# A hybrid attention and convolution block: the second output projection reads convolution features first, and the second attention runs ahead of the first output projection's sums

## The chip, the cores and the metric

The kernel runs on one core of one Trainium2 chip. The time is device time in microseconds (us) of one execution, and the median of several executions is compared. The engines are named as in the profile: PE is TensorE (PEld its weight loads), DVE is VectorE, ACT is ScalarE, POOL is GpSimd, SP is SyncE. SP issues nearly all transfers here; its row in a profile is SPq.

## The reference

One decoder layer of a Hymba-like block, for 2048 positions and a model width of 1024. One input projection feeds two mixers: gated linear attention (4 heads, keys of 64, values of 128, chunks with a state carried from one to the next) and a gated short convolution of width 3. Their outputs, 512 columns each, go side by side through one output projection and are added to the input; then come a gated FFN (width 2816) and a last norm. What matters here, from the reference:

```
h = rmsnorm(x, norm1_g[l]);  proj = h @ w_in[l]
p_q, p_k, p_v, p_g, p_a, c_b, c_c, c_h = jnp.split(proj, splits, axis=-1)
...
o = gla_chunked(q, k, v, log_a)
o = rmsnorm(o, gla_norm_g[l]).astype(x.dtype)
o = o * jax.nn.silu(p_g.reshape(bsz, seq, GLA_HEADS, GLA_DV))
o_gla = o.reshape(bsz, seq, GLA_WIDTH)
u = c_c * c_h
o_conv = c_b * causal_depthwise_conv(u, conv_w[l])
...
x = x + jnp.concatenate([o_gla, o_conv], axis=-1) @ w_out[l]
```

The output projection sums over 1024 input features: eight blocks of 128, of which blocks 0 to 3 are the attention's heads and blocks 4 to 7 the convolution's features.

## The kernel before

**Numbers.** Each float32 operand is split into a high and a low part that TensorE multiplies at its fast rate, and each product of two tiles is three matmuls: high by high (L496), high by low (L497), low by high (L498). The split is an ACT copy (L198) and a DVE subtraction (L199). Most projections use Strassen's seven products on 2 by 2 blocks (`unit`, `PRODUCTS`); their sums are made on DVE (L448, L530, L364) and ACT.

**Tiling.** The 2048 positions are four blocks of 512 columns. Blocks 0 and 1 are the first half, blocks 2 and 3 the second. A matmul is 128x128 by 128x512.

**Stages.** Input projection of the first half, then of the second (`in_proj(1)`, twelve units of seven products), then the first half's output projection (`first_out_proj`), then the second half's (`out_proj`, from 665.57 us in the profiled execution), then the FFN of each half. The first output projection goes through the output rows in four passes, d0 = 0, 2, 4, 6; each makes seven Strassen products on the convolution features and then plain matmuls on the attention heads (L1386, L1392), and adds all to the residual with `plus` (L1355). The second one uses plain matmuls alone (L1421, L1422, L1424). Its operands are 16 tiles `op` of 0.5 MB, eight blocks of features by two blocks of positions, loaded by `build_mix` from `sgla2`, `sgla3` (attention) and `sm2`, `sm3` (convolution); both are stored in DRAM earlier. Each of its weight tiles `raw` is 1 MB, four quarters, and each quarter is split into one of four `wq` buffers. While it runs, `h2_first` makes the norm's factors of the first half's result (sum by ones on PE, L218; root on ACT, L259; refinement on DVE, L261 and L210 to L212) and the FFN's operands from it (L939, L364, L199).

**Work beside the products.** A list `background` of generators is run by `tick()`, which a unit calls once for each product and the output projections at places of their own. It takes one step at every second call. While `hasty` is set, by `hastened(steps, n)` for the first n steps, it takes one at every fourth call besides, so three of four. The attention of a half, `gla_half`, is such a generator. It goes through 8 chunks of 128 positions, in these steps: `gla_fetch` (14 loads: kq, ee, vt, gt), `gla_scaled` (L1161 to L1164), `gla_scores` (PE L1174, masked copy on DVE L1177, transposes L1180, L1183), `gla_outputs` (PE L1199, L1206, L1214; state on DVE L1224, L1225; head norm L1231 to L1240), `gla_finish` (transpose L1249, gate L1250, split, two stores to `sgla`). The first half's attention is `hastened(gla_half(0), 14)` and runs beside the second half's input projection; the second half's is appended in the middle of that projection, after its silu units, and goes on into the first output projection.

**What sets the order.** The program is written in the order of stages and steps, and the framework then sets each engine's order from that program, its own simulation of when things are ready, and the buffers. `behind(marks)` ties an instruction behind others on its engine: with `behind(last_out + last_plus)` an attention split comes behind the last sums that the product loop has written so far. `plus` renews these marks at each sum. SP issues in order, and each transfer waits for the one eight before it. The operand tiles share 28 buffers, so a load of a new tile waits for the matmuls that read an old one.

Of the kernel before, what the change touches and what calls it, by code (L numbers as in the profile page):

```python
# [25 lines left out]
KD = D // P  # L26
# [4 lines left out]
GROUPS = (0, 2, 5, 8)  # L31
LAST_GROUP = GROUPS[-1]
EARLY = 7
EPS = 1e-6


# [17 lines left out]
def tile_hymba_block(ctx, tc, x, xt, win, wa, wgu, wout, wffn, wdown, wdown_first, small, out):  # L54
# [1022 lines left out]
    def in_proj(half, ops, raw=None, between=(), rest=None):  # L1077
        def units():
            if half == 0:
                yield unit(win[2], ops, raw=raw, between=between, rest=rest)  # L1080
            for u in range(0 if half else 3, 12):
                yield unit(win[u], ops, after=2 if half and u < 3 else None)

        units = units()
        for dst, i0 in ((s_kq, 0), (s_kq, 2), (s_v, 0), (s_v, 2)):
            if half == 0 and dst is s_kq:
                continue
            for r, j, c, p in next(units):
                store(dst[2 * half + j][i0 + r][:], settled(c, p)[:])
        for i0 in (0, 2):  # L1090
            for r, j, c, p in next(units):
                store(s_g[2 * half + j][i0 + r][:], silu(c, p)[:])
        if half:
            background.append(gla_half(half))
        for i0 in (0, 2):
            cc = {(r, j): settled(c, p) for r, j, c, p in next(units)}
            ch = {(r, j): c for r, j, c, _ in next(units)}
            for r in range(2):
                i = i0 + r
                left = halo[:, i, :]  # L1100
                for j in range(2):
                    s = tp.tile([P, PB + 2], F32, name="u", tag="t")
                    dve.tensor_tensor(s[:, 2:], ch[r, j][:], cc[r, j][:], ALU.mult)
                    act.activation(s[:, 0:2], left, AF.Copy)
                    left = s[:, PB : PB + 2]
                    y = cc[r, j]
                    act.activation(y[:], s[:, 0:PB], AF.Copy, scale=col(C_CW + i))
                    for n in (1, 2):
                        dve.scalar_tensor_tensor(
                            y[:], s[:, n : n + PB], col(C_CW + 4 * n + i), y[:], ALU.mult, ALU.add  # L1110
                        )
                if half == 0:
                    act.activation(halo[:, i, :], left, AF.Copy)
            for r, j, c, _ in next(units):
                y = cc[r, j]
                dve.tensor_tensor(y[:], c[:], y[:], ALU.mult)
                dst = s_mix[2 * half + j][i0 + r]
                if half:
                    pair_out(y, dst)
                else:  # L1120
                    store(dst[:], y[:])
# [136 lines left out]
    def plain_weights(src, n):  # L1258

        raw = rawp.tile([P, 4, PB], F32, name="raw", tag="raw")  # L1260
        load(raw[:, 0:n, :], src)
        for i in range(n):
            h = weight_quarter(raw[:, i, :])
            for k in range(4):
                yield h[:, 0, k * P : (k + 1) * P], h[:, 1, k * P : (k + 1) * P]
# [69 lines left out]
    def first_out_proj(y, conv, heads):  # L1335

        ssq = [
            tiny.tile([P, PB], F32, name=f"ssx{j}", tag=f"ssx{j}", bufs=1) for j in range(2)
        ]
        for d0 in range(0, KD, 2):  # L1340
            raw = raw_weights(wout[d0 // 2]).rearrange("p a (b e c) -> p (a b) e c", e=2, c=P)
            quads = [raw[:, k : k + 2, e, :] for e, k in ((0, 4), (0, 6), (1, 6), (1, 4))]
            w = unit_weights(None, quads)
            wh = [weight_quarter(raw[:, 0:HEADS, e, :]) for e in range(2)]

            def mul(i, o=None):
                first = o is None
                o = bank() if first else o
                n, m = PRODUCTS[i]
                for k in range(2):  # L1350
                    product_step(o, w[n], conv[m], k, first)
                return o

            def plus(at, o):
                last_plus[:] = [dve.tensor_tensor(y[at][:], o[:], y[at][:], ALU.add)]  # L1355
                last_out[:] = last_plus
                all_plus.extend(last_plus)

            oa = mul(0)
            plus((0, 0), oa)  # L1360
            ob = mul(1)
            plus((1, 1), ob)
            due("T3")
            tick()
            mul(2, oa)
            plus((0, 1), oa)
            due("B22")
            o = mul(3)
            tick()
            mul(4, oa)  # L1370
            plus((1, 1), oa)
            due("T4")
            mul(5, ob)
            plus((0, 1), ob)
            tick()
            mul(6, oa)
            plus((1, 0), oa)
            tick()
            following = residual(d0 + 2) if d0 + 2 < KD else None
            for e in range(2):  # L1380
                po = [bank() if e or j else o for j in range(2)]
                for k in range(HEADS):
                    c = slice(k * P, (k + 1) * P)
                    for j in range(2):
                        for part in range(2):
                            pe.matmul(  # L1386
                                po[j][:], wh[e][:, 0, c], heads[k][j][:, part, :],
                                start=k + part == 0 and e + j > 0, stop=False,
                                skip_group_check=True,
                            )  # L1390
                    for j in range(2):
                        pe.matmul(  # L1392
                            po[j][:], wh[e][:, 1, c], heads[k][j][:, 0, :], start=False,
                            stop=k == HEADS - 1, skip_group_check=True,
                        )
                    if k % 2:
                        tick()
                for j in range(2):
                    plus((e, j), po[j])
                    store(s_x1[j][d0 + e][:], y[e, j][:])  # L1400
                    sum_squares(ssq[j], y[e, j][:], d0 + e == 0)
            y = following
        return ssq

    def build_mix():
        def pair(b, k):
            return load_pair(s_gla[b][:, k] if k < HEADS else s_mix[b][k - HEADS])

        return [[pair(2 + j, k) for j in range(2)] for k in range(KD)]

    def out_proj(ops, ahead, rest):
        ssq, half = [], 1
        ws = chain.from_iterable(plain_weights(wout[u], 4) for u in range(4))
        for d0 in range(0, KD, 2):
            o = {(e, j): bank() for e in range(2) for j in range(2)}
            for k in range(KD):
                for e in range(2):
                    wh, wl = next(ws)
                    for j in range(2):
                        m = ops[k][j]  # L1420
                        pe.matmul(o[e, j][:], wh, m[:, 0, :], start=k == 0, stop=False)  # L1421
                        pe.matmul(o[e, j][:], wh, m[:, 1, :], start=False, stop=False)  # L1422
                    for j in range(2):
                        pe.matmul(  # L1424
                            o[e, j][:], wl, ops[k][j][:, 0, :], start=False, stop=k == KD - 1
                        )
                if k == 3:
                    ys = {}
                    for e in range(2):
                        for j in range(2):  # L1430
                            ys[e, j] = tt("y")
                            load(ys[e, j][:], xt[2 * half + j, :, d0 + e, :])
                for _ in range(1 if d0 == KD - 2 else 2):
                    next(rest if d0 == KD - 2 else ahead, None)
                tick()
            if d0 == 0:
                ssq += [
                    tiny.tile([P, PB], F32, name=f"ssx{j}", tag=f"ssx{j}", bufs=1)
                    for j in range(2)
                ]  # L1440
            for e in range(2):
                for j in range(2):
                    b, dt = 2 * half + j, d0 + e
                    y = ys[e, j]
                    dve.tensor_tensor(y[:], y[:], o[e, j][:], ALU.add)
                    store(s_x1[b][dt][:], y[:])
                    sum_squares(ssq[j], y[:], dt == 0)
        return ssq
# [506 lines left out]
```

## Time and profile before

| | |
|---|---|
| runs (us) | 2042.27, 2048.67, 2047.19 |
| median (us) | 2047.19 |
| the profiled execution (us) | 2047.66 |
| its span (us) | 2045.9 |
| mean granted TensorE clock | 0.995 |
| PE busy | 2021.6 us, 99% |
| DVE, ACT, POOL busy | 76%, 48%, 1% |
| DMA moved | 429.35 MB, 210 GB/s on average |

A line of a wait table gives the waiting engine, tile and line, the releaser, and then total us, number of times and the longest. A row of a timeline is start, duration, engine, line, operation and tiles; "x4" joins neighbours of one kind, and the bracket at its end is the idle time before it and what ended it. A row by windows gives busy us and counts of each engine, then PEclk, the share of full speed that the clock throttle granted, then DMA share and GB/s. Matmuls overlap, so one of 390 ns ends well after the next has begun.

### The profile page before, as it was taken

The numbers are of one execution on the slowest core, as the hardware profiler recorded it, in microseconds if no ns is written. First come the engines' busy times: TensorE is split into PE (matmuls) and PEld (weight loads), VectorE is DVE, ScalarE is ACT, GpSimd is POOL, SyncE is SP. The second block draws the span as 40 slices with busy tenths as digits, with TensorE's granted clock in tenths as the row PEclk, the third lists the DMA queues.
The fourth block names the chain that finished last, engine by engine and source line by source line (L and its number), as shares of the span: only waits on it lengthen the run. The fifth ranks groups of instructions, "written<-read, shape, count | busy, mean of one in ns | idle before, by whom it ended". The sixth has DMA issues, their size and how long they took to land.

```text
span 2045.9 us, 27026 instructions
## 1 busy us (share of the span) xinstructions
PE 2021.6 (99%) x9275; PEld 1658.7 (81%) x9275; DVE 1563.3 (76%) x2837; ACT 973.5 (48%) x1941; POOL 10.3 (1%) x17
## 2 busy tenths in 40 slices
PE   9999999999999999999999999999999999999998
PEld 8788878787877788888888888887888888888886
DVE  7888877668867597778777688887777777778886
ACT  6664455755534244444444453334444444454345
POOL 0000000000000000000000000000000000000001
PEclk9999999999999999999999999999999999999999
DMA  7356886644684893445445576577454444486653
GB/s 262 122 201 220 283 302 190 196 134 157 229 296 160 323 326 140 170 169 207 171 168 195 184 294 240 189 279 294 150 180 170 153 151 170 166 334 226 247 216 129
DMA packets 194634, 429.35 MB, mean 210 GB/s; under 512 B 20448, under 2 KB 67776, under 8 KB 185024
## 3 DMA queue, kind: packets, MB, share of 16 engines
q1 hardware_dynamic: 193776, 426.97, 58.9%
q8 instruction: 73, 1.20, 0.2%
q10 hardware_dynamic: 720, 0.66, 0.1%
q14 instruction: 65, 0.53, 0.1%
HBM read 279.69 MB, written 147.85 MB: 209 GB/s over the span
## 4 chain that ended last, share of the span: by engine, by line
PE 89%; DMA 5%; DVE 3%; ACT 2%; issue 1%; SPq 1%; POOL 0%; POOLq 0%; DVEq 0%; ACTq 0%
PE mm L496 26%; PE mm L498 26%; PE mm L497 26%; PE mm L1421 1%; PE mm L1424 1%; PE mm L1422 1%; DMA raw<-in_win_dram 1%; DMA op<-shT 1%; PE a_ps L1020 1%; PE mm L801 1%; PE mm L803 1%; PE mm L802 1%; PE mm L1741 1%; PE mm L1386 1%; PE o_ps L1199 1%
## 5 line engine op out<-in xcount | busy, mean ns | idle before, releaser
L496 PE MATMUL mm<-op,wq 128*128 128x512 f32 x2499 | 974.3, 393 | 4.1 <-ACT wq L198 1.5
L497 PE MATMUL mm<-op,wq 128*128 128x512 f32 x2499 | 972.3, 390 | 0.6 <-DVE op L199 0.5
L498 PE MATMUL mm<-op,wq 128*128 128x512 f32 x2499 | 962.1, 390 | 0.3
L198 ACT ACTIVATE wq<-raw 128x512 fp32r<-128x512 f32 (+2 forms) x628 | 361.8, 581 | 599.5 <-PE mm L498 477.6
L496 PEld LDWEIGHTS mm<-op,wq 128*128 128x128 f32 x2499 | 469.5, 188 | 107.6 <-ACT wq L198 4.6
L498 PEld LDWEIGHTS mm<-op,wq 128*128 128x128 f32 x2499 | 469.5, 188 | 99.9 <-DVE wq L199 1.9
L497 PEld LDWEIGHTS mm<-op,wq 128*128 128x128 f32 x2499 | 469.8, 188 | 98.6 <-DVE op L199 2.6
L199 DVE TENSOR_TENSOR wq<-raw,wq 128x512 fp32r<-128x512 f32 (+2 forms) x628 | 389.8, 625 | 165.2 <-ACT wq L198 163.6
L530 DVE TENSOR_TENSOR c<-mm,c 128x512 f32<-128x512 f32 x196 | 134.6, 687 | 71.8 <-PE mm L498 67.1
L530 DVE TENSOR_TENSOR y<-mm,y 128x512 f32<-128x512 f32 x185 | 126.5, 687 | 54.1 <-PE mm L498 53.8
L542 ACT ACTIVATE c<-mm 128x512 f32<-128x512 f32 x198 | 115.5, 589 | 33.1 <-PE mm L498 30.6
L448 DVE TENSOR_TENSOR raw<-raw 128x512 f32<-128x512 f32 (+2 forms) x190 | 116.5, 619 | 2.1
L198 ACT ACTIVATE wq<-s 128x512 fp32r<-128x512 f32 (+2 forms) x100 | 58.0, 580 | 101.3 <-PE mm L498 91.5
L448 DVE TENSOR_TENSOR s<-raw 128x512 f32<-128x512 f32 (+2 forms) x95 | 58.9, 620 | 33.9 <-DMA raw<-in_wffn_dram 17.8
L199 DVE TENSOR_TENSOR op<-op 128x512 fp32r<-128x512 f32 x100 | 66.3, 683 | 3.7 <-ACT op L198 3.5
L199 DVE TENSOR_TENSOR wq<-s,wq 128x512 fp32r<-128x512 f32 (+2 forms) x100 | 62.4, 624 | 2.2 <-ACT wq L198 1.4
L198 ACT ACTIVATE op<-op 128x512 fp32r<-128x512 f32 x100 | 59.2, 622 | 9.1 <-DMA op<-siT 3.2
L448 DVE TENSOR_TENSOR raw<-s,raw 128x512 f32<-128x512 f32 (+2 forms) x95 | 59.0, 621 | 1.3
L597 ACT ACTIVATE sg<-mm 128x512 f32<-128x512 f32 x26 | 15.5, 597 | 85.1 <-PE mm L498 85.1
L597 ACT ACTIVATE c<-c 128x512 f32<-128x512 f32 x78 | 48.9, 629 | 13.3 <-DVE c L530 10.6
L1421 PE MATMUL mm<-op,wq 128*128 128x512 f32 x128 | 50.8, 399 | 4.5 <-DMA op<-sgla 4.5
L1422 PE MATMUL mm<-op,wq 128*128 128x512 f32 x128 | 50.5, 395 | 0.0
(240 smaller groups left out, 1689.2 us busy)
## 6 DMA issues: line engine op xcount, KB each, us to landing
raw<-in_wffn_dram SPq DMA_DIRECT2D x44, 1024.0 KB, 5.9
sa_B<-so SPq DMA_DIRECT2D x47, 512.0 KB, 3.7
op<-sa_B SPq DMA_DIRECT2D x47, 512.0 KB, 6.9
raw<-in_win_dram SPq DMA_DIRECT2D x22, 1024.0 KB, 6.0
sa_T<-so SPq DMA_DIRECT2D x44, 512.0 KB, 4.4
op<-sa_T SPq DMA_DIRECT2D x44, 512.0 KB, 6.7
raw<-in_wdown_dram SPq DMA_DIRECT2D x24, 768.0 KB, 5.5
sx<-y SPq DMA_DIRECT2D x48, 256.0 KB, 4.1
```

The costliest lines, as they stand in the source:

```text
L198: last_hi[:] = [act.activation(hi, src, AF.Copy)]
L199: last_lo[:] = [dve.tensor_tensor(lo, src, hi.bitcast(F32), ALU.subtract)]
L448: dve.tensor_tensor(*args)
L496: pe.matmul(o[:], wh, xh, start=first and k == 0, stop=False, skip_group_check=True)
L497: pe.matmul(o[:], wh, xl, start=False, stop=False, skip_group_check=True)
L498: return pe.matmul(o[:], wl, xh, start=False, stop=k == n - 1, skip_group_check=True)
L530: last_plus[:] = [dve.tensor_tensor(t[:], o[:], t[:], ALU.add)]
L542: last_out[:] = [act.activation(t[:], o[:], AF.Copy)]
L597: last_silu[:] = [act.activation(s[:], c[:], AF.Silu)]
L801: pe.matmul(acc[:], wq[:, 0, c], p[:, 0, :], start=first, stop=False)
L1421: pe.matmul(o[e, j][:], wh, m[:, 0, :], start=k == 0, stop=False)
L1422: pe.matmul(o[e, j][:], wh, m[:, 1, :], start=False, stop=False)
```

## The change

Three edits. First, the second output projection takes its eight feature blocks in the order 4, 5, 6, 7, 0, 1, 2, 3: operands are loaded and summed in that order, and the quarters of each weight tile are taken in the order 2, 3, 0, 1. Second, in the first output projection `plus` renews the marks for the background's splits in the pass d0 = 0 alone; later passes leave them where they are. Third, the second half's attention is wrapped in `hastened(..., 9)`.

```diff
+LATE_HEADS = 4, 5, 6, 7, 0, 1, 2, 3
...
         if half:
-            background.append(gla_half(half))
+            background.append(hastened(gla_half(half), 9))
...
         load(raw[:, 0:n, :], src)
-        for i in range(n):
+        for i in (n // 2 + i if i < n // 2 else i - n // 2 for i in range(n)):
             h = weight_quarter(raw[:, i, :])
...
             def plus(at, o):
-                last_plus[:] = [dve.tensor_tensor(y[at][:], o[:], y[at][:], ALU.add)]
-                last_out[:] = last_plus
-                all_plus.extend(last_plus)
+                summed = dve.tensor_tensor(y[at][:], o[:], y[at][:], ALU.add)
+                all_plus.append(summed)
+                if d0 == 0:
+                    last_plus[:] = last_out[:] = [summed]
...
-        return [[pair(2 + j, k) for j in range(2)] for k in range(KD)]
+        return {k: [pair(2 + j, k) for j in range(2)] for k in LATE_HEADS}
...
-            for k in range(KD):
+            for n, k in enumerate(LATE_HEADS):
...
-                        pe.matmul(o[e, j][:], wh, m[:, 0, :], start=k == 0, stop=False)
+                        pe.matmul(o[e, j][:], wh, m[:, 0, :], start=n == 0, stop=False)
...
-                            o[e, j][:], wl, ops[k][j][:, 0, :], start=False, stop=k == KD - 1
+                            o[e, j][:], wl, ops[k][j][:, 0, :], start=False, stop=n == KD - 1
...
-                if k == 3:
+                if n == 3:
```

The set of instructions stays; their order on PE, DVE, ACT and SP is another between the middle of the second input projection and the end of the second output projection (some 485 to 775 us of the profiled execution). Lines of the changed kernel are one further on than before, and two further on in `out_proj`. In the rows that follow a DRAM tile's block number is dropped: sgla_233 and sgla_234 are the attention's results of blocks 2 and 3, sm_0_209 to sm_3_212 the convolution's of block 2, sm_0_213 to sm_3_216 those of block 3, sx the first half's result, stored by output rows.

On SP, at the end of the first output projection and the start of the second, before:

```order
L155 DMA sx_6_175<-y 128x512
L155 DMA sx_6_183<-y 128x512
L155 DMA sgla_234<-gt 512x1x128
L155 DMA sgla_234<-osb 512x1x128
L152 DMA op<-sgla_234 128x1024
L152 DMA op<-sgla_233 128x1024
L152 DMA op<-sgla_234 128x1024
L155 DMA sx_7_176<-y 128x512
L155 DMA sx_7_184<-y 128x512
```

and after:

```order
L156 DMA sgla_234<-gt 512x1x128
L156 DMA sgla_234<-osb 512x1x128
L156 DMA sx_5_174<-y 128x512
L153 DMA op<-sm_3_212 128x1024
L156 DMA sx_5_182<-y 128x512
L153 DMA op<-sm_3_216 128x1024
L153 DMA op<-sgla_233 128x1024
L153 DMA op<-sgla_234 128x1024
```

The last stores of the attention stood behind the sixth residual rows and right ahead of the loads that read them; now they stand ahead of the fifth ones, and two convolution loads come between. The loads of `sgla` behind these rows (two more pairs, a weight tile, one more pair) also stand ahead of sx_6.

On SP, at the start of the first output projection, before, the residual loads followed the last attention store of that place:

```order
L155 DMA sm_3_212<-c_5252 128x512
L155 DMA sgla_233<-gt 512x1x128
L152 DMA y<-in_xt_dram 128x512 x2
L152 DMA raw<-in_wout_dram 128x2048
L152 DMA y<-in_xt_dram 128x512
```

and after, with five convolution loads among them (a sixth follows some 15 rows further on, behind the attention's loads of its next chunk):

```order
L156 DMA sm_3_212<-c_5322 128x512
L156 DMA sgla_233<-gt 512x1x128
L153 DMA op<-sm_0_209 128x1024
L153 DMA op<-sm_0_213 128x1024
L153 DMA op<-sm_1_210 128x1024
L153 DMA op<-sm_1_214 128x1024
L153 DMA y<-in_xt_dram 128x512 x2
L153 DMA op<-sm_2_211 128x1024
L153 DMA y<-in_xt_dram 128x512
L153 DMA raw<-in_wout_dram 128x2048
```

On PE, at the first chunk of the second half's attention, before:

```order
L1180 MATMUL kt_ps<-ident,kq 128x128 x2
L1183 MATMUL v_ps<-ident,vt 128x128 x4
L496 MATMUL mm<-op,wq 128x512
L497 MATMUL mm<-op,wq 128x512
L1199 MATMUL o_ps<-vt,scores 128x128 x2
L1206 MATMUL o_ps<-carry,kq 128x128 x2
```

and after:

```order
L1181 MATMUL kt_ps<-ident,kq 128x128 x2
L1184 MATMUL v_ps<-ident,vt 128x128 x4
L1200 MATMUL o_ps<-vt,scores 128x128 x2
L1207 MATMUL o_ps<-carry,kq 128x128 x2
L497 MATMUL mm<-op,wq 128x512
L498 MATMUL mm<-op,wq 128x512
```

The two product matmuls that stood between the transposes and the attention's outputs now stand behind the outputs.

## The prediction

> **What bounds the kernel now.** I read the page's totals first, then PE's waits, then stretches of time by engine, then the timelines around the two longest waits.
>
> ```profile
> span 2045.9 us, 27026 instructions
> PE 2021.6 (99%) x9275; PEld 1658.7 (81%) x9275; DVE 1563.3 (76%) x2837; ACT 973.5 (48%) x1941; POOL 10.3 (1%) x17
> PE 89%; DMA 5%; DVE 3%; ACT 2%; issue 1%; SPq 1%; POOL 0%; POOLq 0%; DVEq 0%; ACTq 0%
> ```
>
> PE is busy for 99% of the span and carries 89% of the chain that ended last. Time is won here only by fewer matmuls, by waits of PE that go, or by a higher granted clock. The change leaves the set of matmuls as it is, so what counts is PE's waits (columns: total, times, longest, us):
>
> ```profile
> PE mm L1421 <- DMA op<-sgla: 4.5, 1, 4.5
> ...
> PE o_ps L1199 <- ACT c L542: 2.1, 1, 2.1
> ...
> PE v_ps L1183 <- issue: 1.4, 1, 1.4
> ...
> PE mm L1386 <- DMA op<-sgla: 0.4, 1, 0.4
> ```
>
> All four lie between 486 and 671 us, in the stretch whose order the change rewrites. The granted clock is below 1.00 in two of the windows there (columns: PE, PEld, DVE, ACT, POOL busy with counts, PEclk, DMA share, GB/s):
>
> ```profile
> 450.00:500.00 50.00, 47.77 (x211) 37.93 (x210) 44.43 (x86) 31.38 (x71) 0.00 (x0) 0.93 0.45 149
> 650.00:700.00 50.00, 45.46 (x190) 36.22 (x189) 21.23 (x38) 12.26 (x22) 0.00 (x0) 0.93 0.77 278
> ...
> 665.50:689.50 24.00, 19.46 (x73) 14.78 (x72) 8.65 (x14) 6.14 (x10) 0.00 (x0) 0.86 0.95 349
> 689.50:713.50 24.00, 24.00 (x107) 19.89 (x106) 15.43 (x25) 7.34 (x13) 0.00 (x0) 1.00 0.83 298
> ```
>
> The last two rows are the start and the next part of the second output projection: the same kind of matmul, 73 of them in 24 us and then 107. So each takes 24/107 = 0.224 us at full clock.
>
> **The change part by part.** The sum is made on the profiled execution, 2047.66 us, which is 0.47 us above the median of the three runs, 2047.19 us.
>
> *1. Convolution features first, and the attention's last splits untied.* This is the long wait, on PE and on SP's queue:
>
> ```profile
> 665.57 0.39 PE L1421 MATMUL mm<-op,wq 128*128 128x512 f32 x1
> ...
> 666.03 0.39 PE L1424 MATMUL mm<-op,wq 128*128 128x512 f32 x1
> 670.95 0.80 PE L1421 MATMUL mm<-op,wq 128*128 128x512 f32 x1 [4.54 <-DMA op<-sgla]
> ```
> ```profile
> 663.24 0.52 SPq L155 DMA_DIRECT2D sgla<-osb  x1
> 665.85 1.28 SPq L152 DMA_DIRECT2D op<-sgla  x3
> ...
> 672.47 8.45 SPq L152 DMA_DIRECT2D op<-sm  x8
> ```
>
> The attention's last result is stored at 663.24, the loads that need it go out from 665.85, and the first lands near 670.9, while PE wanted it at 666.4. Idle time: 4.54 us. Then the clock:
>
> ```profile
> 671.00:675.50 4.50, 4.50 (x10) 3.42 (x11) 0.00 (x0) 0.00 (x0) 0.00 (x0) 0.50 1.00 381
> 675.50:680.00 4.50, 4.50 (x18) 3.02 (x17) 2.95 (x5) 3.59 (x5) 0.00 (x0) 0.99 1.03 409
> ```
>
> It stood at half until 675.5: 8 matmuls fewer in 4.5 us than in the next 4.5, some 2.0 us. So this stall costs at least 4.54 + 2.0 = 6.5 us; by the count of 24 us it is 34 x 0.224 = 7.6 us at most, since four of the 73 are sums of the norm, which take longer than the others. I take the middle, **-7.1**.
>
> After the change the first 48 matmuls of this stage (10.8 us at 0.224) read convolution features, which were stored before the first output projection began. Six of their eight loads stand in SP's order at the start of that projection, among its residual loads; the other two and the eight attention loads in its last block, behind the last stores of sgla3, which now stand ahead of the stores of the fifth and sixth residual rows instead of behind them. Ten loads of the kind in the row of x8 take 10 x 8.45/8 = 10.6 us in the queue, and a weight load of twice the size, ahead of the last two, 2.1 more. If they start no later than the end of the last block they arrive beside the 10.8 us of convolution matmuls and the first attention ones; they stand in front of that block's own sx stores, so they start earlier. I count no wait; bounds for what is left of this stall, 0 to 2.2 us (half of the old idle time).
>
> The sum of the norm (L218) stands 48 matmuls later, too, so the second norm's chain on DVE starts later after the stage's start:
>
> ```profile
> 677.05 0.69 DVE L261 TENSOR_SCALAR rb<-tot 128x512 f32<-128x512 f32 x1 [8.41 <-ACT l L259]
> ...
> 690.14 0.69 DVE L199 TENSOR_TENSOR wq<-raw,wq 128x512 fp32r<-128x512 f32 x1 [7.53 <-ACT wq L198]
> 696.26 0.69 DVE L199 TENSOR_TENSOR wq<-raw,wq 128x512 fp32r<-128x512 f32 x1 [5.43 <-ACT wq L198]
> 699.45 0.69 DVE L1445 TENSOR_TENSOR y<-y,mm 128x512 f32<-128x512 f32 x1 [2.50 <-PE mm L1424]
> 700.06 0.74 DVE L939 SCALAR_TENSOR_TENSOR h<-h,sml,rb 128x512 f32<-128x512 f32 x1
> ```
>
> Between its rb at 677 and its first h at 700, DVE sat through three waits of 15.5 us behind weights and sums that stood in between. Now the h instructions follow rb directly, so they begin no later than before, counted from the stage's start. Cost 0, hidden by those 15.5 us; if the cover failed, the first FFN unit would wait for its operands, a few us.
>
> *2. Attention at 3 of 4 products for its first nine steps.* One more chunk comes before the first output projection, so its inputs and stores are earlier. The nearest row for that pace is the first half's attention, which ran at it:
>
> ```profile
> 278.00:430.00 152.00, 151.79 (x836) 122.06 (x835) 104.67 (x228) 93.84 (x224) 0.00 (x0) 1.00 0.63 199
> 485.00:560.00 75.00, 72.77 (x368) 57.90 (x367) 57.13 (x124) 41.24 (x107) 0.00 (x0) 0.95 0.59 203
> ```
>
> PE sat idle for 0.2 us of 152 there, with DVE 69% busy. The second half has DVE at 76% already at 2 of 4. So the new waits lie between 0.2 us and one more stall like the one below (5.4 us). I take **+0.5**, near the first, since the same steps ran beside the same kind of unit.
>
> The start of this attention has the second stall:
>
> ```profile
> 488.18 1.19 PE L1199 MATMUL o_ps<-vt,scores 128*128 128x128 f32 x4 [2.15 <-ACT c L542]
> ...
> 487.60 0.77 DVE L1177 COPY_PREDICATED scores<-mask,sc 128x256 f32<-128x256 uint32 x2
> ...
> 488.20:494.70 6.50, 6.50 (x18) 5.18 (x19) 4.52 (x9) 1.42 (x4) 0.00 (x0) 0.50 0.40 153
> 494.70:501.20 6.50, 6.50 (x35) 4.88 (x35) 2.93 (x6) 3.10 (x11) 0.00 (x0) 1.00 0.48 166
> ```
>
> PE waits for the masked copy of the scores (until 488.0), which is late in DVE's queue, and then runs 6.5 us at half clock: 2.15 + 6.5/2 = 5.4 us. The same work stands ahead of that copy on DVE and ACT after the change, but two matmuls fewer on PE (in its order they come behind o_ps now), so PE arrives 2 x 0.224 earlier and waits that much longer: **+0.45**. Bounds: +0.45 with the clock as it is, -3.2 if the clock stays full this time.
>
> [...]
>
> *3. Smaller waits in the first output projection.*
>
> ```profile
> 612.88 0.42 DVE L448 TENSOR_TENSOR s<-raw 128x256 f32<-128x256 f32 x1 [4.26 <-DMA raw<-in_wout_dram]
> ...
> 615.39 0.63 PE L1183 MATMUL v_ps<-ident,vt 128*128 128x128 f32 x4 [1.39 <-issue]
> 616.36 0.47 PE L496 MATMUL mm<-op,wq 128*128 128x512 f32 x1 [0.33 <-DVE osb L1240]
> ```
>
> DVE sat for a weight load and PE lost 1.39 + 0.33 us behind it. The load now stands ahead of attention loads that it stood behind, and its first use is later in DVE's order: between 0 and -1.72, I take **-1.2**. The wait of 0.4 us at L1386 comes from an attention load in the queue, which an earlier chunk eases: between 0 and -0.4, **-0.2**.
>
> Against this, the early convolution loads take 8.45/8 = 1.06 us of the queue each: four of them (4.2 us) stand ahead of the second residual tile, five (5.3 us) ahead of the next weights and attention inputs. PE reaches those later by one chunk of attention:
>
> ```profile
> L1199 PE MATMUL o_ps<-vt,scores 128*128 128x128 f32 x64 | 9.6, 288 | 2.1 <-ACT c L542 2.1
> L1206 PE MATMUL o_ps<-carry,kq 64*128 64x128 f32 x64 | 9.4, 317 | 0.0
> L1174 PE MATMUL sc<-kq 64*128 64x128 f32 x56 | 5.5, 299 | 0.0
> L1249 PE MATMUL ot<-ident,osb 128*128 128x128 f32 x32 | 5.3, 272 | 0.0
> L1183 PE MATMUL v_ps<-ident,vt 128*128 128x128 f32 x30 | 4.7, 275 | 1.5 <-issue 1.4
> L1214 PE MATMUL kv<-vt,ee 128*64 128x128 f32 x56 | 4.6, 285 | 0.0
> L1180 PE MATMUL kt_ps<-ident,kq 128*128 128x128 f32 x14 | 3.0, 294 | 0.0
> ```
>
> These are the busy sums of the eight chunks (485 to 665 us), 42.1/8 = 5.3 us for one, which covers the loads' 4.2 to 5.3. Bounds: 0 to 5.3 us late, at three places; taken as 0.
>
> Sum: 2047.66 - 7.1 + 0.5 + 0.45 - 1.2 - 0.2 = 2040.1 us for an execution like the profiled one; 0.47 less for a median is 2039.6. I give **2040.0**, between the two.
>
> **The rivals.**
>
> *The clock stays full at the first stall.* Whether a gap near 2 us halves it may depend on where the gap falls against the clock's own steps; one of the three runs, 2042.27, is 4.9 us under the median, the size of such a step with a little idle time. Time: 2040.1 - 3.2 = 2036.9. Against it: the gap becomes longer, 2.6 us. [...]
>
> *The denser attention makes DVE the bound before 560 us.* One chunk more there adds to 57.13 busy us of 75, and the window with the stall had 44.43 of 50. One more stall like it gives 5.4 us back: 2045.5, within 0.3%; three of them end above 2053. For it: the 89% of that window. Against it: 0.2 us in 152.
>
> *Slower: the early loads hold up the first output projection.* One mechanism, the backlog in SP's queue near 575 us. If PE is not later by a chunk, the second residual tile is 4.2 us late and the next weights and inputs 5.3. A wait of 4.26 us on DVE cost PE 1.72, so cover is 2.5 us: 1.7 + 2.8 + 2.8 us of idle PE at residual, weights and attention input, and 3.2 of half clock behind the two longer ones: 2040.1 + 7.3 + 6.4 = 2053.8. It decides from 2.5 us late on. Against it: the chunk's 5.3 us.
>
> *The change doesn't do what it says.* The last stores come no earlier, or a convolution load is as late as the attention load was: the stall stays, 2047 to 2048.
>
> **How the numbers follow.** Forecast 0.50 (own range 2037.5 to 2043.5), full clock at the first stall 0.17, DVE bound 0.16, backlog 0.10, nothing done 0.07. About 0.3%, 6.1 us, is what a measurement can tell from no change: faster is below 2041.05, slower above 2053.3. Of the forecast 0.38 lie below and 0.12 within; the full clock's 0.17 below; of DVE's 0.12 within, 0.04 above; the backlog above; of the last 0.06 within, 0.01 above. Faster 0.55, same 0.30, slower 0.15. The range, 2034.5 to 2049.5, leaves out the upper DVE cases and the backlog, and a little below.
>
> **What would show it.** Right: no wait at L1423 on sgla or sm, clock 1.00 there, some 107 matmuls in each 24 us of that stage; the last sgla3 stores some 20 us before it; the wait at o_ps still there, 2.6 us long. Wrong: a new wait of PE above 1.5 us between 490 and 600 us with half clock behind it, DVE over 90% in a window there, y or raw loads landing after DVE wants them, or the FFN's first unit waiting for operands.

## The result

The changed kernel took 2039.52 us (median of 7 runs, 2038.44 to 2042.86) and the kernel before 2046.37 (7 runs): a ratio of 0.9970, 95% interval 0.9959 to 0.9982. Measured a second time beside other kernels it was 2041.21 against 2046.84, 0.9979 (0.9969 to 0.9990). So it is 0.2 to 0.3% faster, 5.6 to 6.9 us by the two pairs of medians. The profiled execution took 2038.44 us, 9.2 us below that of before (2047.66); it is the fastest of its seven runs and that of before one of the slower ones, so the two traces differ by more than the medians do.

PE's waits in the profile after, those that belong to the second attention and the output projections:

```profile
PE o_ps L1200 <- ACT c L543: 3.0, 1, 3.0
...
PE v_ps L1184 <- DMA vt<-sv: 1.1, 1, 1.1
...
PE mm L1388 <- DMA op<-sgla: 0.8, 1, 0.8
...
PE sc L1175 <- DVE kq L1165: 0.4, 1, 0.4
```

The wait of 4.5 us of the second output projection's matmuls on `sgla` is gone. The waits of the attention and the first output projection are still there, and the longest of them, at o_ps, grew by 0.8 us. By windows (PE, PEld, DVE, ACT, POOL busy with counts, then PEclk, DMA share, GB/s):

```profile
450.00:500.00 50.00, 47.04 (x214) 37.73 (x214) 46.17 (x96) 32.53 (x76) 0.00 (x0) 0.93 0.45 151
...
490.00:560.00 70.00, 70.00 (x382) 56.01 (x383) 53.27 (x119) 39.52 (x110) 0.00 (x0) 0.98 0.62 208
...
650.00:700.00 50.00, 50.00 (x218) 40.74 (x217) 35.15 (x56) 17.41 (x28) 0.00 (x0) 1.00 0.84 299
...
663.00:687.00 24.00, 24.00 (x104) 19.18 (x103) 15.67 (x25) 8.71 (x14) 0.00 (x0) 1.00 0.67 221
687.00:711.00 24.00, 24.00 (x108) 19.87 (x107) 21.78 (x36) 9.50 (x17) 0.00 (x0) 1.00 0.94 324
```

From 650 to 700 us PE is never idle and has the full clock, and the first 24 us of the second output projection hold 104 matmuls where there were 73. SP's timeline shows that the operands are there in time:

```profile
640.34 0.53 SPq L156 DMA_DIRECT2D sgla<-gt  x1
641.16 0.52 SPq L156 DMA_DIRECT2D sgla<-osb  x1
643.43 0.33 SPq L156 DMA_DIRECT2D sx<-y  x1
643.85 0.38 SPq L153 DMA_DIRECT2D op<-sm  x1
...
645.30 3.39 SPq L153 DMA_DIRECT2D op<-sgla  x6
649.76 0.33 SPq L153 DMA_DIRECT2D raw<-in_wout_dram  x1
650.76 1.59 SPq L153 DMA_DIRECT2D op<-sgla  x2
```

The last attention store goes out at 641.16, 22 us before that projection begins (663.14), and all its operand loads are issued by 652.4.

The gain by stages, from the starts of matmuls in the two traces (us):

| stage | before | after | difference |
|---|---|---|---|
| up to the second attention's first scores | 483.70 | 483.10 | -0.60 |
| from there to the second output projection | 181.88 | 180.04 | -1.84 |
| second output projection | 95.79 | 88.81 | -6.98 |
| FFN to the last matmul's end | 1278.26 | 1278.42 | +0.16 |

The third row comes out alike in every trace: the stage took 88.81 us in each kernel that removes its stall. The second row is not: a second trace of the changed kernel took 183.85 us there, and a kernel that differs from the one before only behind that stage took 180.04. So the -1.84 is no larger than what one program scatters.

### The profile page after: what moved, and what is told of

Its sections match the earlier page's. It is cut to its first block, busy times and chain, and to the rows that moved or that the text cites. A ratio compares the mean times of both kernels' runs of the same rounds, so it can differ in the third digit from the quotient of the medians.

```text
span 2036.7 us, 27040 instructions
## 1 busy us (share of the span) xinstructions
PE 2016.2 (99%) x9275; PEld 1656.8 (81%) x9275; DVE 1565.9 (77%) x2837; ACT 975.5 (48%) x1941; POOL 10.3 (1%) x17
## 4 chain that ended last, share of the span: by engine, by line
PE 91%; DMA 4%; DVE 3%; ACT 1%; issue 1%; SPq 0%; POOL 0%; POOLq 0%; DVEq 0%; ACTq 0%
PE mm L497 26%; PE mm L499 26%; PE mm L498 26%; PE mm L1423 1%; PE mm L1424 1%; PE mm L1426 1%; PE mm L1388 1%; DMA op<-shT 1%; DMA op<-siT 1%; PE a_ps L1021 1%; PE mm L802 1%; PE mm L804 1%; PE mm L803 1%; PE mm L1743 1%; PE o_ps L1200 1%
```

## The experiments

All times are medians beside runs of the kernel before on the same chip; the ratio is to those, with its 95% interval.

**Each edit alone.** First edit, convolution features first:

```diff
...
-            for k in range(KD):
+            for n, k in enumerate(LATE_HEADS):
...
```

> Only the first edit: convolution features first, the marks and the attention's pace as before. Theory (the 4.54 us stall is the distance from the last sgla3 store to the first matmul that reads it, and either a later first read or an earlier last store removes it): PE's wait on sgla goes, since the first such matmul stands 48 matmuls (10.8 us) later; clock 1.00 there; the first stall near 486 us stays as before at 2.1 us; 7 us faster than before, so about 2039.5. Rival (the earlier attention does it, the order of the features only moves the wait): a wait of over 2 us on sgla at the 49th matmul of the stage with half clock behind it, 2044 or more.

2039.16 us against 2047.19: 0.9963 (0.9951 to 0.9976). The second output projection took 88.81 us and waited for no operand; the first stall stayed at 2.2 us. The last attention store still went out late, and so did the loads behind it, as SP's rows show; PE runs through all the same (the row by windows), so here it is the later first read that removes the stall.

```profile
661.09 0.52 SPq L156 DMA_DIRECT2D sgla<-osb  x1
663.76 1.27 SPq L153 DMA_DIRECT2D op<-sgla  x3
```
```profile
663.40:687.40 24.00, 24.00 (x103) 19.16 (x102) 12.88 (x20) 8.02 (x12) 0.00 (x0) 1.00 0.92 328
```

The theory held and the rival fell: this edit alone gives, within the intervals, as much as all three.

Second edit, the splits untied:

```diff
-                last_plus[:] = [dve.tensor_tensor(y[at][:], o[:], y[at][:], ALU.add)]
-                last_out[:] = last_plus
...
+                if d0 == 0:
+                    last_plus[:] = last_out[:] = [summed]
```

> Only the second edit: the splits untied from the later sums. Theory: the attention keeps its pace of two in four, so its last step comes where it came before; the last sgla3 store moves by no more than a row or two in SP's order, and the stall stays within 1 us of 4.5: 2045 to 2047.5. Rival (the ties held the last splits back by several us): the wait on sgla falls under 2 us, 2040 to 2043.

2044.93 us: 0.9984 (0.9975 to 0.9993). Between the two theories: the wait was halved, not kept and not gone.

```profile
667.14 0.39 PE L1425 MATMUL mm<-op,wq 128*128 128x512 f32 x1
669.85 0.78 PE L1422 MATMUL mm<-op,wq 128*128 128x512 f32 x1 [2.32 <-DMA op<-sgla]
```

The ties had held the last splits back by some 2 us: the last store now goes out 4.5 us before the projection begins, where it was 2.3. That I expected no more than 1 us of it was wrong.

Third edit, the pace:

```diff
-            background.append(gla_half(half))
+            background.append(hastened(gla_half(half), 9))
```

> Only the third edit: the second attention at three of four products for nine steps. Theory: the last sgla3 store comes some 15 us before the stage, the attention loads in time, the convolution loads behind them one by one: no wait above 0.5 us there, clock 1.00; the first stall 0.45 to 0.8 us longer than before; 6.5 us faster than before, about 2040. Rival (the order of the features is what counts): 16 loads in the last block don't arrive in time, a wait on sgla or sm of 2 us or more, 2044 or more.

2041.15 us: 0.9974 (0.9962 to 0.9985). The second output projection again took 88.81 us, without a wait, heads first and all sixteen loads in time. So two of the edits remove the same stall, each by itself. But the pace has a price elsewhere, in the first output projection:

```profile
574.17 0.73 PE L1386 MATMUL mm<-op,wq 128*128 128x512 f32 x2 [3.02 <-DMA op<-sgla]
```

In the kernel before, this wait is 0.44 us long.

**How the stall splits into idle time and clock.** Extra matmuls in the idle time of the kernel before:

```diff
                     wh, wl = next(ws)
+                    if d0 == 0 and k == 0 and e == 0:
+                        for _ in range(18):
+                            pe.matmul(o[0, 0][:], wh, ops[0][0][:, 0, :], start=True, stop=True)
```

> The kernel before with 18 extra matmuls ahead of the second output projection's first one, into the bank that the first one then starts anew; the result is not changed. They take 18 x 0.224 = 4.0 us and lie in the wait of 4.54 us. Theory (the half clock behind the stall comes from PE's idle time, and costs 2.0 to 3.0 us): PE stays busy, clock 1.00 from 668 to 676 us, a wait of 0.5 us left, 2.0 to 3.0 us faster than before: about 2043.9. Rival (the clock falls there for another reason, or the 7 us are idle time alone): no faster, 2046 to 2047.

2045.46 us: 0.9992 (0.9984 to 1.0001), unclear by the time alone. The trace tells more. PE runs through but for 0.26 us, and the clock stays at 1.00 where the stall was:

```profile
664.47 4.24 PE L1421 MATMUL mm<-op,wq 128*128 128x512 f32 x18
...
669.64 0.50 PE L1424 MATMUL mm<-op,wq 128*128 128x512 f32 x1 [0.26 <-DMA op<-sgla]
```
```profile
668.60:676.00 7.40, 7.14 (x28) 4.90 (x27) 2.39 (x4) 3.03 (x5) 0.00 (x0) 1.00 1.00 357
```

The second output projection took 93.73 us with the 18 matmuls, 95.79 without them: doing more work in the gap saved 2.06 us. What is left above 88.81 us, 4.92, is the 4.07 us of the added matmuls, the wait of 0.26 and some 0.6 more. The trace of before splits its own stall, 95.79 - 88.81 = 6.98 us, into 4.54 of idle time and 2.44 of the rest, so the clock's share lies between 2.06 and 2.44 us. The half clock goes with the idle time here: with 0.26 us of it the clock stayed at 1.00, with 4.54 us it fell to 0.50. The first stall, 2.1 us, which this kernel leaves as it was, still has it.

**Two edits of three,** each as a step back from the changed kernel. Heads first again:

```diff
...
-            for n, k in enumerate(LATE_HEADS):
+            for k in range(KD):
...
```

> The second and third edits, heads first as before. The pace alone took the stall at the second output projection away (its span 88.81 us, as in the whole change) but brought a wait of 3.0 us at L1386 near 572 us. Theory (the early convolution loads of the first edit are not needed where the attention ends early): span of that projection 88.8 us, 2040 to 2042, the wait at L1386 still 1 to 3 us since it comes from the pace. Rival (that wait comes from the order of the loads that untying sets): under 0.5 us, 2038 to 2039.

2041.43 us: 0.9971 (0.9962 to 0.9979). As the theory had it: 88.81 us, with a wait of 2.9 us at L1387.

Ties as before, the other two edits kept:

```diff
...
-                if d0 == 0:
-                    last_plus[:] = last_out[:] = [summed]
+                last_plus[:] = [dve.tensor_tensor(y[at][:], o[:], y[at][:], ALU.add)]
+                last_out[:] = last_plus
```

> The first and third edits, the splits tied as before. Theory (the stall goes by either of these two, the untying adds nothing on top): within 1.5 us of the whole change, 2038 to 2041. Rival (untying is what keeps the denser attention's splits from being late): a wait over 1 us between 570 and 660 us, 2042 or more.

2042.51 us: 0.9977 (0.9967 to 0.9987). Above the theory's 2041, and the rival's wait is there, 2.5 us at L1387. But the same wait stands in the kernels with the pace whose splits are untied, so it is not the ties that make it.

Pace as before, the other two kept:

```diff
-            background.append(hastened(gla_half(half), 9))
+            background.append(gla_half(half))
```

> The first and second edits, the attention at two of four as before. Theory: the stall at the second output projection is gone as with the first edit alone (span 88.8 us), and the wait at the attention's start stays 2.1 us, 0.8 less than in the whole change: 2037.5 to 2039.5, not slower than the whole change. Rival (the pace adds a gain of its own): 2040.5 or more.

2041.56 us: 0.9967 (0.9955 to 0.9979), with a spread from 2036.29 to 2042.27 over six runs. The stall is gone (88.81 us), the first stall is 2.1 us, and the wait at L1388 is 0.5 us. The median is above what I expected and falls on the rival's side; the ratio is close to that of the first edit alone. The ratios of all kernels so far that remove the stall lie between 0.9963 and 0.9979 and their intervals overlap; these runs don't order them.

**The first stall.** I had read it as a wait for DVE's masked copy. In this kernel the attention's output matmuls are tied behind the products written before them:

```diff
-            o = gla_outputs(b, t, *s)
+            o = gla_outputs(b, t, *s, products[-1:] if half and n == 0 else ())
...
+                with behind(marks):
                     pe.matmul(
                         o[e][:, i, :], scores[:, h, :], v[:, h, :], start=i == 0, stop=first,
```

> The whole change, and in the second attention's first chunk the matmuls of its outputs tied behind the products that the program writes before them: twelve product matmuls (2.7 us) then stand between the transposes and o_ps. Theory (the 3 us wait there is PE arriving before the masked copy, and the half clock comes from that idle time): the wait falls to 0.3 us or less, clock 1.00 near 490 us, 2.7 us of idle time and 1.5 to 3.2 of half clock saved: 2033.6 to 2035.5. Rival (DVE is the bound there, and PE waits as long a little later): 2038 to 2040.

2039.82 us: 0.9961 (0.9949 to 0.9973). The theory fell. The rival's wait came, as long as before and now at a product, but PE waits for ACT and not for DVE (PE's row, then ACT's queue up to the release):

```profile
488.30 0.65 PE L498 MATMUL mm<-op,wq 128*128 128x512 f32 x1 [2.95 <-ACT c L545]
```
```profile
484.20 1.67 ACT L200 ACTIVATE wq<-raw 128x512 fp32r<-128x512 f32 x3 [1.13 <-DVE raw L450]
...
486.62 1.14 ACT L200 ACTIVATE hi<-c 128x512 fp32r<-128x512 f32 x2
487.66 1.07 ACT L545 ACTIVATE c<-mm 128x512 f32<-128x512 f32 x2
```

A product needs no scores, so the masked copy can't be what it waits for. PE's results go to buffers of the PSUM memory, and products and the attention's outputs take theirs from one pool of eight (tag "mm"). By the row of 488.30 PE's next output needed the buffer that ACT's copy c<-mm empties, and the copy stands behind three weight splits, the attention's copies and two splits for the convolution stores. The next kernel takes those two splits off ACT, with two more of the same stores:

```diff
+        if on_pool:
+            last_hi[:] = [pool.tensor_copy(hi[:], y[:])]
+            last_lo[:] = [dve.tensor_tensor(y[:].bitcast(F32R), y[:], hi[:].bitcast(F32), ALU.subtract)]
...
```

> As held_outputs, and the four high parts of the first convolution stores (hi<-c, two of them right ahead of the copies c<-mm on ACT) are made on POOL. In held_outputs PE still waited 3.0 us, now a product matmul for ACT's copy c<-mm, so my reading of the first stall (DVE's masked copy) was at best half of it. New theory: PE has no free PSUM bank until ACT has copied a product out, and ACT is late by its queue. The two splits take 0.52 us each: the wait falls from 3.0 to about 1.9 us, the clock may then stay at 1.00; 2036 to 2039.5. Rival (the copy waits for something else than ACT's queue): still 2.8 us or more, no change against held_outputs.

2038.68 us: 0.9964 (0.9952 to 0.9977).

```profile
485.89 1.08 ACT L545 ACTIVATE c<-mm 128x512 f32<-128x512 f32 x2
```
```profile
486.54 0.50 PE L498 MATMUL mm<-op,wq 128*128 128x512 f32 x1 [1.94 <-ACT c L545]
```
```profile
486.50:493.40 6.90, 6.86 (x40) 5.38 (x41) 6.63 (x13) 3.57 (x12) 1.60 (x2) 1.00 0.64 238
```

The copy comes right after the attention's copies, the wait is 1.94 us instead of 2.95, as worked out from the two splits' time, and the clock stays at 1.00 in this execution. So ACT's queue sets the length of this stall: 1.04 us taken out of it made the wait 1.01 us shorter. That is shown in the trace alone; the time doesn't tell the two kernels apart (0.9964 and 0.9961). In the changed kernel itself the same rows stand ahead of the same copy, which ends at 487.54, and PE goes on at 487.57.

**The wait that the pace brought.** The first output projection's operand loads for the second to fourth head stand in SP's queue behind the 14 loads of one attention chunk, and PE waits for the second head's. That is so in the kernel before, too. What the pace adds is one more chunk earlier in the queue: from the attention's first scores to the second head's first load SP issues 93 transfers instead of 77; of the 16 more, 14 are loads of that chunk and two are stores of results. With the third edit alone that load lands 4.75 us later than before (574.13 against 569.38), and PE comes only 2.2 us later. Here POOL issues the 14 right ahead of it:

```diff
-                load(dst[:, i, :], r[:, s])
+                (nc.gpsimd.dma_start if (b, t) == (3, 1) else load)(dst[:, i, :], r[:, s])
```

> The whole change, and the 14 small loads of one attention chunk (the one fetched near 555 us, ahead of the first output projection's attention operands) are issued by POOL instead of SP. Theory (the wait of 0.8 to 3.2 us at the first output projection's first attention matmul comes from SP's queue: the operand loads stand behind these 14, which take 12 us to issue): the operand loads go out early, no wait there above 0.2 us and no half clock there; 1 to 4 us less than the whole change, 2036 to 2038.5. Rival (the operands wait for free buffers, not for the queue): the wait stays, 2039 to 2041.

2045.42 us: 0.9995 (0.9984 to 1.0005). No gain is left. The second head's first load goes out at 556.4 and lands at 566.7, where the whole change had 567.6 and 572.7, and its matmuls no longer wait; so the queue was the cause there. But the loads of the four heads land no closer than 1.2 us apart, and two new waits come:

```profile
572.36 0.73 PE L1388 MATMUL mm<-op,wq 128*128 128x512 f32 x2 [1.13 <-DMA op<-sgla]
576.03 1.22 PE L1175 MATMUL sc<-kq 64*128 64x128 f32 x8 [2.70 <-issue]
```
```profile
574.09 0.63 ACT L1270 ACTIVATE ssx<-y 128x512 f32<-128x512 f32 x1 [2.89 <-DVE y L1356]
574.62 0.40 ACT L1162 ACTIVATE ee<-ee 128x256 f32<-128x256 f32 x1
```

The first is for the fourth head's load (landed 572.32). The second is order: with the loads elsewhere the order of the engines' work was set anew, the attention's decay factors (L1162) came behind ACT's square of a sum that PE's late matmuls had yet to make, and PE waited 2.70 us for the scores' input. Changing who issues a load changed more than that load.

Both edits together:

> Both of the edits of held_pool and fetch_pool together. Theory: their gains add, 2033 to 2037. Rival (each only moves a wait): 2038.5 or more.

2039.32 us: 0.9970 (0.9958 to 0.9981), so the gains don't add, as the rival had it. Its trace has the same two new waits, 1.08 and 2.71 us, with half clock for 6.8 us as in the kernel with the loads on POOL alone. So these two waits don't account for that kernel's lost gain, and what does is open.

The whole change once more:

> The whole change once more, beside the three others on one chip. Expected: 2039 to 2041, with the wait at the first output projection's first attention matmul anywhere between 0.5 and 3.2 us from execution to execution, if it is the queue's.

2041.21 us, 2038.88 to 2047.17 in 11 runs, just above what I expected. Its profiled execution took 2045.7 us, 7.3 more than the first one of the same kernel, and the two traces show where. The wait for the second head's operands is 2.86 us, with half clock behind it, where it was 0.77; and one in the FFN, for a split on ACT that itself waited 2.62 us for a load (0.80 in the first trace), has grown in the same way:

```profile
575.62 0.73 PE L1388 MATMUL mm<-op,wq 128*128 128x512 f32 x2 [2.86 <-DMA op<-sgla]
...
1401.92 0.50 PE L497 MATMUL mm<-op,wq 128*128 128x512 f32 x1 [2.19 <-ACT op L199]
```

In the first trace the FFN's wait is 0.37 us long; with the first edit alone it is 2.87. No experiment tried to hold these loads' times still.

## Why the prediction was right, and where it was not

The predicted 2040.0 us lies between the two measured medians, and its sum rests on one term that was right; most of the small terms were not. They came to -0.45 us. By the medians the gain was 5.6 to 6.9 us, so what came beside the stall's -6.98 was +0.1 to +1.4 us. In the two traces it was -2.3 and +5.0. That the number is so near is in part luck: the small terms missed in both directions.

- **The stall at the second output projection, -7.1.** Measured -6.98 in the stage; the bounds were 6.5 and 7.6. The clock's share, put at 2.0 or more, was 2.06 to 2.44. What the prediction did not see is that two of the three edits each remove the whole stall: "convolution features first, and the attention's last splits untied" were costed together, and the earlier loads were put down to the pace as well. The untying alone halves it. The gain of the three is not a sum.
- **The norm's chain on DVE, 0.** Right. The first h came at 680.09, 17 us after the stage began (34.5 before), directly behind rb, and the FFN took as long as before.
- **The first stall, +0.45.** The step "PE waits for the masked copy of the scores, which is late in DVE's queue" failed. The row named ACT's copy c, L542, as the releaser; I set it aside for a DVE instruction that ended 0.1 us earlier. The two kernels above show that ACT's queue holds it. The wait grew by 0.8 us (2.15 to 2.96), not 0.45, and is 2.9 to 3.0 in each of the kernels with the pace where PE comes to these matmuls first. The lower bound, -3.2, had left out that longer wait; with it, it was -2.8.
- **New waits of the denser attention, +0.5, and the wait at L1386, -0.2.** Together they were put at +0.3. The second has the wrong sign: this wait is the one that grew, by 0.3 us in the first trace after and by 2.4 in the second, and no other new one above 0.5 us came in either. That the first trace fits is luck. The step "which an earlier chunk eases" failed: the chunk that comes earlier puts its own loads and stores into SP's queue ahead of the operand loads, and delays them by more than it delays PE. In six of the seven profiles with the pace and all loads on SP it is 2.4 to 3.2 us long with the clock at half behind it, and 0.8 in the first profile of the whole change. So one of the signs named for being wrong, a new wait above 1.5 us between 490 and 600 us with half clock behind it, did come in the second trace of the changed kernel. It is a backlog in SP's queue, but not the one of the rival: the two kernels with the pace and without the early convolution loads wait as long, 3.0 and 2.9 us. At the places that the rival had priced, DVE waited 1.54 us for a residual tile and 2.59 for weights in the first trace after, where it had been 3.05 and 4.26; so no cost of the early loads, taken as 0, shows there.
- **The wait after DVE's idle time, -1.2.** 1.1 us of wait is left at v_ps, now for a load of vt, and 0.45 at sc: -0.2 in place of -1.2, though DVE's wait for the weights became 1.7 us shorter.
- **What is not accounted for.** In the stage between the attention's start and the second output projection PE's idle time rose from 4.5 to 5.3 us, but the stage became 1.84 us shorter in that trace. Some 2.6 us less busy time follows; half clock at the first stall is about 0.3 of it (5.9 us of busy time at half clock, 6.5 before). The rest lies in matmuls that follow each other more closely in another order. Counted from each matmul's start to the next one's, without idle time and half clock, o_ps takes 1.2 us less, mm 0.7 and v_ps 0.4, and the second trace of the changed kernel agrees; no experiment tried it apart.

The rival "the clock stays full at the first stall" came in none of the kernels that keep that stall's length: twelve profiles with a wait of 2.1 us or more there all had half clock. The DVE-bound rival (a second stall before 560 us) did not come: from 490 to 560 us PE was never idle in the profile after (the row above), with DVE busy for 53.27 us of 70.

## What to carry to other kernels

Before adding up the parts of a change, ask for each what is left of the stall once another part is in: two ways to remove one wait are worth one wait, and the second brings only its own costs, here a load queue that comes late in the stage before. Where the profile names a releaser that ended within a tenth of a microsecond of the one that the story wants, take a little out of each one's queue before believing either. Two traces of one program differed here by 7.3 us, because two waits for loads grew, from 0.77 to 2.86 us and from 0.37 to 2.19, and half clock stood behind both; so a stage of one trace against the same stage of another shows a gain only where it comes out alike in several.

## What the runs showed of the hardware

- At the first stall all twelve waits of 2.1 to 3.0 us were followed by half clock, for 3.4 us in five profiles and for 6.8 us in seven (in the one before from 487.85 to 494.67, in the one after from 486.67 to 493.50). A wait of 1.94 us was once not followed by it (the row of 486.50 above) and a wait of 1.95 us was, in the kernel with both edits:

```profile
488.10:491.40 3.30, 3.30 (x9) 2.55 (x9) 3.30 (x8) 0.00 (x0) 0.73 (x2) 0.50 0.62 240
```

- When the granted clock changed. In the profile before it did so at 487.85, 494.67, 668.75 and 675.58 us, 6.83, 174.08 and 6.83 us apart, and in the one after at 486.67 and 493.50, 6.83 apart: 2, 51, 2 and 2 times 3.413 us. Count on from these moments in steps of that length, and a row for each step has PE's idle time in it (the length less PE's busy time). Three rows before and one after:

```profile
484.44:487.85 3.41, 1.51 (x8) 0.84 (x8) 3.41 (x8) 3.41 (x9) 0.00 (x0) 1.00 0.84 276
614.14:617.56 3.42, 1.83 (x9) 1.47 (x10) 3.39 (x13) 1.91 (x6) 0.00 (x0) 1.00 0.68 209
665.34:668.76 3.42, 1.07 (x5) 0.56 (x3) 3.09 (x5) 1.67 (x3) 0.00 (x0) 1.00 0.55 118
```
```profile
483.26:486.67 3.41, 1.36 (x14) 1.00 (x14) 3.41 (x8) 3.18 (x8) 0.00 (x0) 1.00 0.79 256
```

Of the steps at full clock between 100 and 2010 us in these two profiles, the three with the most idle time, 1.90, 2.35 and 2.05 us, were followed by half clock, and the next one, with 1.59 us (the row of 614.14), was not. In the two kernels with a wait just under 2 us, the gap of 1.94 us fell on two steps, with 1.26 and 0.68 us of idle time, and the one of 1.95 us into one (two rows of the first kernel, then one of the second):

```profile
482.44:485.86 3.42, 2.16 (x18) 1.41 (x16) 3.42 (x9) 2.38 (x6) 2.03 (x2) 1.00 0.81 278
485.86:489.27 3.41, 2.73 (x11) 2.10 (x12) 3.41 (x8) 1.12 (x3) 2.24 (x2) 1.00 0.81 294
```
```profile
484.62:488.03 3.41, 1.47 (x9) 0.96 (x9) 3.41 (x8) 3.08 (x8) 2.05 (x1) 1.00 0.75 253
```

This fits the rival's guess that what a gap near 2 us does depends on where it falls; no more than these two gaps speak for it.

- Behind the stall of 4.54 us the clock was at half for 6.8 us (668.75 to 675.58), but 2.2 of these were still the gap; half clock cost 2.06 to 2.44 us there.
